# The first mixer's rotation without a product, and inverse-sum rows by transposition, in a two-block transformer kernel

## The chip, the cores and the metric

The kernel is one program on one core of a Trainium2 chip. The metric is the time of one execution on the device in microseconds (us), the median over runs. One core has a tensor engine (PE, whose loads of stationary operands are listed apart as PEld), a vector engine (DVE), a scalar engine (ACT), GpSimd (POOL) and a sync engine (SP), which here issues the transfers between memories (DMAs). All engines take their instructions in order and wait for each other through semaphores.

## The reference

A transformer of two blocks works on 512 tokens of 1024 features, and on 256 context tokens in its first block. The first block has two layers, each an attention mixer with adaptive gains (adaLN); the second block has two layers, each a mixer and a convolutional feed-forward part. The change touches three mixers.

The first mixer (mixer_a) has 16 heads of 64 features that share four key/value heads. Queries and keys of the latent tokens are rotated; those of the context are not:

```python
def apply_rope(x, cos, sin):
    a1, a2, b1, b2 = jnp.split(x, 4, axis=-1)
    rot = jnp.concatenate([-a2, a1, -b2, b1], axis=-1)
    return x * cos + rot * sin

# mixer_a, for each block of 128 queries
s_loc = q . k (three key blocks, window of 128) * scale
s_ctx = q . kc (256 context keys, not rotated) * scale
p = softmax([s_loc, s_ctx, sink])
y = (p v * silu(g)) @ w_o
```

The second mixer (mixer_b, 16 heads, latent attention) and the first mixer of the second block (even_mixer, 8 heads of 64 beside a linear recurrence) end in a division of each query's output by its row sum of exponentials; the kernel does it after the product with V.

## The kernel before

Matrices are kept transposed, with features on the 128 rows (partitions) and tokens on columns. Each float32 operand of a large product is split into a high and a low part (fp32r), and a product is three products of parts (`gemm_T`). Products that are not split are float32 products and stand in the trace as two records each.

The planner of the language orders each engine's instructions itself, by priority (the order of the program text) and by its own estimate of when operands are ready; buffers and PSUM banks go by tags. In the first mixer the banks are two for projections ("pj"), two for transpositions ("tp"), three for scores ("S") and one for outputs ("po").

`attn_a` (stage A1, about 64 to 412 us of the trace) is the first mixer. `g_k(pr)` and `g_q(t)` project a pair of heads for 512 latent tokens (bank `px`) and 256 context tokens (bank `pc`); both are pj banks, so a projection takes both. `rope` (line 559) rotates `px`: with a matrix `rot` ACT copies px to SBUF (`sw`), PE multiplies `sw` by the constant 128x128 matrix `rot` into a tp bank, and DVE multiplies that by the sine table, `sw` by the cosine table, and adds. Without a matrix (mixer_b and even_mixer, whose rotated partners lie 64 rows apart) ACT copies each half of 64 rows of px to the other half, and DVE multiplies px by the cosines, the copy by the signed sines, and adds. The result is split into `tH` and `tL` (128x768), of which SP moves the rows of each head by DMA (`dcopy`, line 591) into `Q` or `K`: in `g_q` two DMAs of 64 rows for each of two heads, in `g_k` four. `rope` is called 10 times in `attn_a`: for two pairs of keys and eight of queries. `head_a` then makes scores, softmax, transposed probabilities and outputs; `merge` interleaves a head's scores, the outputs of the head before, and projections (`g_q`, `g_g`, `g_v`, and chunks of the adaLN weights, `ada_...`) that fill PE in between and take pj banks as well.

`rows` (line 613) turns four columns of inverse row sums [128, 1] into rows [64, 128]: four float32 products whose stationary operand is the column repeated 64 times and whose moving operand is the identity. `head_b` (stage B3, about 590 to 800 us) calls it once for each of 16 heads, and `head_e` through `o_sum` (stage E, about 940 to 1050 us) once for each of 8. DVE reads the result from the tp bank.

`dhead` (line 600), used by even_mixer, moves one head out of a tile whose rotated halves lie 64 rows apart: two DMAs of 32 rows.

Of the kernel before, what the change touches and what calls it, by code (L numbers as in the profile page):

```python
# [43 lines left out]
# ---------------------------------------------------------------- host layout  # L44
def _tiles(w, groups):
    """[K, N] -> one [128, K/128 * 128] block per group of columns (features of a chunk on rows)."""
    kc = w.shape[0] // P
    w3 = w.reshape(kc, P, w.shape[1])
    return np.stack([np.ascontiguousarray(w3[:, :, g].transpose(1, 0, 2)).reshape(P, -1) for g in groups])


def _nat(w, ksub, cols):
    """[K, N] -> blocks [128, ksub * cols], ordered column chunk, then rows."""
# [23 lines left out]
def _rotmat(d, n):  # L77
    """lhsT of the axial rotation: out[m] = sum_p r[p, m] q[p]."""
    r = np.zeros((d, d), np.float32)
    q = d // 4  # L80
    for a, b in ((0, 1), (2, 3)):
        for i in range(q):
            r[b * q + i, a * q + i] = -1.0
            r[a * q + i, b * q + i] = 1.0
    return np.kron(np.eye(n, dtype=np.float32), r)


def _halves(d, n, axial):
    """order of the columns of n heads of d features in which each rotated pair lies n * d / 2 columns apart."""
    q = d // 4  # L90
    one = np.arange(d).reshape(2, 2, q).transpose(1, 0, 2) if axial else np.arange(d).reshape(2, 1, 2 * q)
    return (one.reshape(2, 1, d // 2) + d * np.arange(n)[None, :, None]).reshape(-1)


def _rope_rows(c, s, n, axial):
    """cos and signed sin tables [n * d, 2 S] for columns in that order."""
# [6 lines left out]
def _consts():  # L103
# [7 lines left out]
    c["rope_a"] = np.concatenate([np.tile(ca.T, (2, 1)), np.tile(sa.T, (2, 1))], 1)  # L111
    c["rot_a"] = _rotmat(64, 2)
# [20 lines left out]
def _layout(x):  # L133
# [12 lines left out]
    a["a_k"] = _tiles(w, [1024 + np.arange(P * i, P * i + P) for i in range(2)])  # L146
    a["a_v"] = _nat(w[:, 1280:1536], 4, 256)
    a["a_q"] = _tiles(w, pair)
# [63 lines left out]
# ---------------------------------------------------------------- the program  # L212
def blk(x, b):
    """token block b of a transposed operand, kept whole or as two halves."""
# [15 lines left out]
def some(g, n):  # L230
    """the next n steps of g."""
# [5 lines left out]
def skew(gs, lag=2):  # L237
    """Second halves of the generators some turns after the first ones."""
# [12 lines left out]
def mix(*gs):  # L251
    """Interleave generators; a third one (projections) takes four steps to the others' one."""
# [18 lines left out]
class Prog:  # L271
# [16 lines left out]
    # ---- small wrappers  # L288
# [18 lines left out]
    def bcast(self, ap, pool, n, tag, bufs=1):  # L307
        """[n] in DRAM -> [128, n]."""
# [4 lines left out]
    def gemm_T(self, W, toks, off=0, kc=8):  # L313
        """out^T tiles: weights stationary; toks: [(X, n, psum ap)]."""
# [8 lines left out]
    def gemm_first(self, srcs, pss, X, ahead=50):  # L323
        """The first output tiles of a phase, in halves of the tokens: the first half needs only the
        first two blocks, and goes ahead of the last block's norm."""
# [7 lines left out]
    def rstd(self, ms, n=1):  # L333
        """(ms)^-0.5 on [128, n]."""
# [4 lines left out]
    def sq(self, x, ss, f):  # L339
        """mean square of half f of a [128, 1024] tile's rows."""  # L340
# [5 lines left out]
    def row_r(self, x, ss=None):  # L346
        """1 / rms of a [128, 1024] tile's rows."""
# [7 lines left out]
    def norm_T(self, x, X, b, ps, acol, bcol=None, ss=None):  # L355
        """x: [128, 1024] token block -> columns of block b of X = (H list, L list), by a gain alone (a row
        of features on all partitions) or by gain and shift columns; the last step, out of the transposes,
        is left to the next call, so that its chain goes first."""
# [37 lines left out]
    def turn(self, n=0):  # L396
        """the transposes of norm_T that are open, but for the last n."""
# [21 lines left out]
    def out_proj(self, W, nch, X, nblk, ps, consume, first=None, late=0, begun=None):  # L419
        """natural out: activations stationary, weights moving; W[g * nch + i] = [128, 2k, 512]."""  # L420
# [33 lines left out]
    # ---- adaLN columns  # L454
# [28 lines left out]
    def ada_chunk(self, l, c, pm, row=0, full=None, fs=()):  # L483
        """512 columns; parts H, L of c go to rows row, 32 + row, those of c_ctx to 64 + row, 96 + row.
        Some chunks go unsplit by float32 products with full, where the tensor engine has the time."""
# [21 lines left out]
    def ada_cols(self, l, half, ps, tag, pool, full=None, fs=()):  # L507
        """gain and shift columns of half of the features, for the latents and the context."""
# [23 lines left out]
    def ada_grow(self, l, c, ps, tag):  # L532
        """rows of half a gate, added to the tile that holds the rows of all of them."""
# [10 lines left out]
    def ada_gates(self, l, c, ps, gates):  # L544
        """half c of the gates: [two [128, 512] halves for the latents (and the context)]."""
# [12 lines left out]
    # ---- pieces shared by the attentions  # L558
    def rope(self, ps_q, pool, tab, rot=None):
        """psum [128, 512] -> rotated [128, 512] f32 in SBUF; partners lie 64 rows apart, or come by a product  # L560
        with the constant rot."""
        nc = self.nc
        sw = self.t(pool, [P, S], F32, "tmp", 3)
        if rot is not None:
            self.act(sw, ps_q)
            pr = self.bank("tp")
            self.mm(pr, rot, sw, start=True, stop=True)
            t2 = self.t(pool, [P, S], F32, "tmp", 3)
            nc.vector.tensor_mul(t2, pr, tab[:, S:])
            nc.vector.tensor_mul(sw, sw, tab[:, :S])  # L570
            nc.vector.tensor_add(sw, sw, t2)
            return sw
# [16 lines left out]
    def dcopy(self, out, in_):  # L589
        """f32r rows moved between partitions."""  # L590
        self.nc.sync.dma_start(out.bitcast(F32), in_.bitcast(F32))

    def pv(self, po, cols, v, pH, pL, kb, last):
        """P V of key block kb into columns cols: rows 0-63 (V's high part) and 64-127 are to be added."""
# [1272 lines left out]
```

## Time and profile before

| | |
|---|---|
| median of 3 runs | 2120.14 us (2115.47 to 2120.24) |
| span of the profiled execution | 2120.9 us |
| PE busy | 2046.0 us, 96% |
| DVE busy | 1294.2 us, 61% |
| ACT busy | 1055.6 us, 50% |
| DMA engines | 34.1% of 16 engines' span |

The page gives no time of the profiled execution besides its span. The span is 0.8 us above the median of the runs. The busy time of PE includes the modelled ends of pipelined products, so 96% does not say that PE is at its peak.

### The profile page before, as it was taken

To read this page: it belongs to the slowest core of one execution; us is meant where nothing else is said; L and a number is where in the kernel's file an instruction comes from. 1 tells how busy PE (TensorE), PEld (TensorE's weight loads), DVE (VectorE), ACT (ScalarE), POOL (GpSimd) and SP (SyncE) were. 2 spreads that over 40 slices of the span, in tenths; PEclk is the share of its full clock that TensorE was granted. 3 is DMA by queue.
4 is the path that set the end of the run, shared out by engine and by line. 5 is a ranking of instruction groups with operands and counts; after the bars stand their busy time and mean duration, and the time that the engine had idled before them with its cause. 6 is when DMAs were issued, how large, how long until landed. Compare 5 with 4: busy or idle time off the path is not lost.

```text
span 2120.9 us, 28788 instructions
## 1 busy us (share of the span) xinstructions
PE 2046.0 (96%) x10609; PEld 1692.5 (80%) x10609; DVE 1294.2 (61%) x2491; ACT 1055.6 (50%) x2044; POOL 74.4 (4%) x162
## 2 busy tenths in 40 slices
PE   7899999998999999999999999999999999999998
PEld 4778888777788877867778888887888878888886
DVE  5588788847488886657756444423666775444323
ACT  5377677725367664555534333322566754333321
POOL 2100000000000000000000000000000000000000
PEclk9999999999999999999999999999999999999999
DMA  7344423322334332232123222222565532322222
GB/s 261 102 129 135 115 85 91 113 82 78 120 91 109 86 95 80 94 100 60 40 100 109 100 100 95 95 95 84 138 158 153 139 119 100 100 100 93 96 95 84
DMA packets 80893, 223.65 MB, mean 105 GB/s; under 512 B 13408, under 2 KB 19312, under 8 KB 80752
## 3 DMA queue, kind: packets, MB, share of 16 engines
q1 hardware_dynamic: 80752, 221.81, 34.1%
q8 instruction: 84, 1.38, 0.3%
q14 instruction: 57, 0.47, 0.1%
HBM read 176.67 MB, written 4.19 MB: 85 GB/s over the span
## 4 chain that ended last, share of the span: by engine, by line
PE 82%; DVE 7%; ACT 5%; issue 2%; DMA 2%; POOL 2%; SPq 0%; POOLq 0%; ACTq 0%; DVEq 0%
PE pj L293 33%; PE S L293 28%; PE po L293 13%; PE tp L293 2%; DVE wL L304 2%; PE tp L1305 1%; PE tp L1100 1%; POOL rstd L336 1%; ACT wH L290 1%; DVE XL L584 1%; ACT tmp L290 1%; ACT junk L290 1%; PE tp L1786 1%; PE tp L375 1%; DVE nm L1293 1%
## 5 line engine op out<-in xcount | busy, mean ns | idle before, releaser
L304 DVE TENSOR_TENSOR wL<-raw,wH 128x1024 fp32r<-128x1024 f32 (+2 forms) x291 | 353.9, 1220 | 461.7 <-ACT wH L290 449.1
L290 ACT ACTIVATE wH<-raw 128x1024 fp32r<-128x1024 f32 (+2 forms) x291 | 305.5, 1053 | 540.8 <-PE S L293 216.1
L293 PE MATMUL pj<-XH,wH 128*128 128x512 f32 (+1 forms) x672 | 260.5, 391 | 3.8 <-ACT tmp L290 1.3
L293 PE MATMUL pj<-XL,wH 128*128 128x512 f32 (+1 forms) x672 | 259.9, 390 | 0.1
L293 PE MATMUL pj<-XH,wL 128*128 128x512 f32 (+1 forms) x672 | 257.6, 386 | 0.5 <-DVE wL L304 0.5
L293 PE MATMUL S<-K,Q 96*128 96x384 f32 (+4 forms) x864 | 190.7, 330 | 4.5 <-ACT P L290 3.1
L293 PE MATMUL S<-XH,wH 128*128 128x512 f32 (+1 forms) x456 | 170.2, 374 | 1.0 <-ACT wH L290 1.0
L293 PE MATMUL S<-XH,wL 128*128 128x512 f32 (+1 forms) x456 | 169.9, 373 | 0.5 <-DVE wL L304 0.5
L293 PE MATMUL S<-XL,wH 128*128 128x512 f32 (+1 forms) x456 | 170.0, 373 | 0.0
L293 PEld LDWEIGHTS S<-K,Q 128*128 128x128 f32 (+1 forms) x864 | 141.8, 189 | 20.2 <-ACT P L290 7.2
L293 PEld LDWEIGHTS pj<-XH,wH 128*128 128x128 f32 x672 | 127.0, 189 | 29.7 <-ACT wH L290 2.7
L293 PEld LDWEIGHTS pj<-XH,wL 128*128 128x128 f32 x672 | 127.1, 190 | 23.3 <-issue 1.2
L293 PEld LDWEIGHTS pj<-XL,wH 128*128 128x128 f32 x672 | 127.4, 190 | 22.7 <-issue 1.8
L290 ACT ACTIVATE PTH<-tp 128x512 fp32r<-128x512 f32 (+2 forms) x192 | 91.2, 480 | 40.4 <-PE tp L1100 15.7
L584 DVE TENSOR_TENSOR PTL<-tp,PTH 128x512 fp32r<-128x512 f32 (+2 forms) x192 | 103.4, 542 | 9.3 <-ACT PTH L290 8.4
L293 PEld LDWEIGHTS S<-XH,wH 128*128 128x128 f32 x456 | 86.1, 189 | 16.4 <-ACT wH L290 1.7
L293 PEld LDWEIGHTS S<-XH,wL 128*128 128x128 f32 x456 | 86.3, 189 | 16.0 <-DVE wL L304 1.0
L293 PEld LDWEIGHTS S<-XL,wH 128*128 128x128 f32 x456 | 86.3, 189 | 15.1
L290 ACT ACTIVATE XH<-tp 128x512 fp32r<-128x512 f32 x128 | 75.1, 596 | 43.3 <-PE tp L375 24.0
L584 DVE TENSOR_TENSOR XL<-tp,XH 128x512 fp32r<-128x512 f32 x128 | 86.7, 684 | 10.6 <-ACT XH L290 9.5
L290 ACT ACTIVATE P<-S,nm 128x768 f32<-128x768 f32 (+1 forms) x96 | 72.5, 757 | 31.4 <-DVE nm L1018 12.2
L293 PE MATMUL po<-PTH,V 128*128 128x256 f32 (+1 forms) x224 | 79.0, 356 | 2.2 <-ACT PTH L290 2.0
(482 smaller groups left out, 4519.3 us busy)
## 6 DMA issues: line engine op xcount, KB each, us to landing
raw<-in_up SPq DMA_DIRECT2D x88, 512.0 KB, 3.4
raw<-in_ada SPq DMA_DIRECT2D x48, 512.0 KB, 4.3
raw<-in_dn SPq DMA_DIRECT2D x44, 512.0 KB, 3.4
raw<-in_o_o SPq DMA_DIRECT2D x11, 512.0 KB, 3.8
x<-in_x SPq DMA_DIRECT2D x8, 512.0 KB, 9.1
raw<-in_a_q SPq DMA_DIRECT2D x8, 512.0 KB, 4.6
raw<-in_a_g SPq DMA_DIRECT2D x8, 512.0 KB, 3.7
raw<-in_a_o SPq DMA_DIRECT2D x8, 512.0 KB, 3.5
```

Of the source, the lines that this page charges most:

```text
L290: self.nc.scalar.activation(out, in_, func, **kw)
L293: self.nc.tensor.matmul(out, l, r, start=start, stop=stop, **kw)
L304: nc.vector.tensor_sub(L[:, :n], raw[:, :n], H[:, :n].bitcast(F32))
L336: self.nc.gpsimd.tensor_tensor(r, ms, self.c_mh[:, :n], op=ALU.pow)
L375: nc.tensor.transpose(tp[:, kk, :], xh[g][:, kk * P:(kk + 1) * P], self.ident)
L584: self.nc.vector.tensor_sub(L, src, H.bitcast(F32))
L1100: nc.tensor.transpose(tp[:, (i - i0) * P:(i - i0 + 1) * P], Ps[i][0][:, at(i) * P:(at(i) + 1) * P], self.ident)
L1293: nc.vector.tensor_reduce(nm[:, i:i + 1], Sp[:, :, :384], axis=AX.XY, op=ALU.min)
L1305: nc.tensor.transpose(tp[:, i * P:(i + 1) * P], Ps[i][:, kb * P:(kb + 1) * P], self.ident)
L1786: nc.tensor.transpose(tp[:, (i - kb) * P:(i - kb + 1) * P], Ps[i][0][:, kb * P:(kb + 1) * P], self.ident)
```

## The change

The columns of the first mixer's query and key weights are reordered on the host, so that the partners of each rotated pair come out 64 rows apart, as in the other two rotated mixers; the table `rope_a` is laid out for that order, with the sign in the sine part. `rope` loses its branch with the matrix, and the constant `rot_a` and its DMA go. `g_k` and `g_q` move heads by `dhead`, so that each DMA of 64 rows becomes two of 32 rows. `rows` calls the transposition of PE where it called a product with the identity. Comments and docstrings are removed as well.

```diff
-    c["rope_a"] = np.concatenate([np.tile(ca.T, (2, 1)), np.tile(sa.T, (2, 1))], 1)
-    c["rot_a"] = _rotmat(64, 2)
+    c["rope_a"] = _rope_rows(ca, sa, 2, True)
...
-    a["a_k"] = _tiles(w, [1024 + np.arange(P * i, P * i + P) for i in range(2)])
+    ro = _halves(64, 2, True)
+    a["a_k"] = _tiles(w, [1024 + P * i + ro for i in range(2)])
-    a["a_q"] = _tiles(w, pair)
+    a["a_q"] = _tiles(w, [p[ro] for p in pair])
...
-    def rope(self, ps_q, pool, tab, rot=None):
+    def rope(self, ps_q, pool, tab):
         nc = self.nc
         sw = self.t(pool, [P, S], F32, "tmp", 3)
-        if rot is not None:
-            self.act(sw, ps_q)
-            pr = self.bank("tp")
-            self.mm(pr, rot, sw, start=True, stop=True)
-            t2 = self.t(pool, [P, S], F32, "tmp", 3)
-            nc.vector.tensor_mul(t2, pr, tab[:, S:])
-            nc.vector.tensor_mul(sw, sw, tab[:, :S])
-            nc.vector.tensor_add(sw, sw, t2)
-            return sw
         for z in (0, 64):
             self.act(sw[z:z + 64], ps_q[64 - z:128 - z])
         qs = self.t(pool, [P, S], F32, "tmp", 3)
...
         bc = self.bank("tp")
         for i in range(n):
-            self.mm(bc[0:64, i * P:(i + 1) * P], r[:, i:i + 1].to_broadcast([P, 64]), self.ident, start=True, stop=True)
+            self.nc.tensor.transpose(bc[0:64, i * P:(i + 1) * P], r[:, i:i + 1].to_broadcast([P, 64]), self.ident)
         return bc
...
-        rot = self.t(pool, [P, P], F32, "rot", 1)
-        nc.sync.dma_start(rot, I["rot_a"])
...
-            kf = self.rope(px, pool, rope, rot)
+            kf = self.rope(px, pool, rope)
...
-                        self.dcopy(k2[64 * hf:64 * hf + 64, i, :], src[64 * e:64 * e + 64, :])
+                        self.dhead(k2[64 * hf:64 * hf + 64, i, :], src, e)
...
-            qf = self.rope(px, pool, rope, rot)
+            qf = self.rope(px, pool, rope)
...
-                self.dcopy(q2[0:64, :], qH[64 * e:64 * e + 64, :])
-                self.dcopy(q2[64:128, :], qL[64 * e:64 * e + 64, :])
+                self.dhead(q2[0:64, :], qH, e)
+                self.dhead(q2[64:128, :], qL, e)
```

## Rows read from the trace of the kernel before

**Rows 1.** The page: chain that ended last, share of the span by engine and line

```profile
PE 82%; DVE 7%; ACT 5%; issue 2%; DMA 2%; POOL 2%; SPq 0%; POOLq 0%; ACTq 0%; DVEq 0%
```

**Rows 2.** Stretches: length, busy us (instructions) PE PEld DVE ACT POOL, clock, DMA, GB/s

```profile
260.00:280.00 20.00, 20.00 (x120) 17.39 (x118) 17.04 (x41) 13.56 (x32) 0.83 (x3) 1.00 0.25 69
...
590.00:800.00 210.00, 204.82 (x1214) 172.62 (x1213) 179.63 (x276) 145.95 (x290) 0.00 (x0) 1.00 0.37 95
...
940.00:1050.00 110.00, 107.38 (x663) 85.02 (x662) 81.64 (x212) 65.88 (x166) 2.72 (x3) 0.97 0.20 58
```

**Rows 3.** Chain within stage B3 (590 to 800 us), share by line

```profile
by line: PE S L293 22.4%; PE po L293 19.6%; PE tp L1305 14.7%; PE pj L293 11.9%; PE tp L293 7.7%; DVE nm L1293 5.2%; ACT tmp L290 3.4%; DVE XL L584 2.9%; issue 2.9%; ACT P L290 2.7%; DVE tmp L1321 2.3%; ACT XH L290 1.7%; DVE OT L1322 1.3%; 
```

**Rows 4.** PE groups, forms apart: out<-in, shape, count, busy us, mean ns, idle before

```profile
L293 PE MATMUL tp<-ident,l 128*64 128x128 f32 x128 | 18.0, 280 | 0.0
...
L293 PE MATMUL tp<-tmp,rot 128*128 128x512 f32 x20 | 10.8, 624 | 1.3 <-ACT tmp L290 1.3
L293 PE MATMUL tp<-ident,rl 128*64 128x128 f32 x64 | 10.2, 300 | 0.0
```

**Rows 5.** Timeline of PE at one call of rows in B3: start, duration, instruction

```profile
656.64 0.40 PE L293 MATMUL po<-XL,V 128*128 128x512 f32 x1
656.97 1.09 PE L293 MATMUL tp<-ident,l 128*64 128x128 f32 x8
...
658.33 0.34 PE L293 MATMUL S<-K,Q 96*128 96x384 f32 x1
```

**Rows 6.** Timeline of PE at four transpositions in B3

```profile
604.88 0.34 PE L293 MATMUL S<-K,Q 96*128 96x384 f32 x1
...
605.07 0.60 PE L1305 MATMUL tp<-ident,P 128*128 128x128 f32 x4
...
605.74 0.40 PE L293 MATMUL pj<-cqH,wL 128*128 128x512 f32 x1
```

**Rows 7.** Timeline of weight loads: a 32-column transposition (L1158) behind a 128-column one

```profile
511.48 0.14 PEld L1157 LDWEIGHTS tp<-ident,xhc 128*128 128x128 f32 x1
511.54 0.10 PEld L1158 LDWEIGHTS tp<-ident,xhc 128*32 128x32 f32 x1
```

**Rows 8.** Timeline of PE at one rotation product in A1

```profile
139.37 0.34 PE L293 MATMUL po<-PTL,V 128*128 128x384 f32 x1
139.55 0.34 PE L293 MATMUL po<-PTH,V 128*128 128x384 f32 x1
139.84 1.10 PE L293 MATMUL tp<-tmp,rot 128*128 128x512 f32 x2
...
141.01 0.40 PE L293 MATMUL pj<-wL,adast 128*128 128x512 f32 x1
141.25 0.39 PE L293 MATMUL pj<-wH,adast 128*128 128x512 f32 x1
```

**Rows 9.** Timeline of DVE and ACT at another rope in A1

```profile
274.57 1.23 DVE L304 TENSOR_TENSOR wL<-raw,wH 128x1024 fp32r<-128x1024 f32 x1 [0.92 <-ACT wH L290]
274.70 0.59 ACT L290 ACTIVATE tmp<-pj 128x512 f32<-128x512 f32 x1
```

**Rows 10.** DVE's cosine product without a matrix, ACT's copies: ns min/median/max

```profile
L576 DVE TENSOR_TENSOR tmp<-pj,rope_e x5: 681/690/691, 916.7 to 1019.6; 128x512 f32<-128x512 f32 x5
...
L290 ACT ACTIVATE tmp<-pj x31: 577/590/624, 65.5 to 1073.2; 64x512 f32<-64x512 f32 x16, 128x512 f32<-128x512 f32 x15
```

**Rows 11.** SP's issues: 64-row DMAs in A1, 32-row DMAs in E

```profile
84.28 1.11 SPq L591 DMA_DIRECT2D Q<-tL  x2
...
953.03 1.15 SPq L591 DMA_DIRECT2D Q<-tH  x2
```

**Rows 12.** What PE waited for, 64 to 412 us: total us, times, longest

```profile
PE tp L293 <- ACT tmp L290: 1.3, 1, 1.3
```

**Rows 13.** Around a fall of the granted clock in A1: PE's gap, and the stretch behind

```profile
241.61 1.05 PE L293 MATMUL tp<-sel,sgx 128*128 128x2 f32 x8 [0.96 <-ACT sgx L290]
...
244.00:248.00 4.00, 4.00 (x18) 3.39 (x17) 3.28 (x8) 3.12 (x6) 0.00 (x0) 0.61 0.17 41
```

More of the change, by code (lines that the diff above doesn't have):

```diff
@@ L74, in _axial @@
     return np.cos(ang).astype(np.float32), np.sin(ang).astype(np.float32)
[L77 to L85, printed above, removed]
 def _halves(d, n, axial):
```

## The prediction

> **What bounds the kernel now.** I read the page's chain first: most of the span is on PE [rows 1]. Then the stages that the change touches, by stretches [rows 2]: in A1 PE is busy in all of a 20 us stretch, in B3 in 204.8 of 210 us, in E in 107.4 of 110, at the full granted clock or near it. DVE comes second: 85% of A1's stretch, 179.6 of 210 us in B3, 74% of E. So PE is the bound, but with little room above DVE in A1 and B3. The chain within B3 says the same in another way: its PE lines make up 76%, DVE and ACT take turns for most of the rest, and the line "tp L293" (7.7% of 210 us, 16.2 us, about 1.0 us for each of 16 heads) is the products of `rows` themselves: they lie on the chain [rows 3]. The time of a PE instruction can't be taken from its listed duration, which holds the modelled end; I take the distance between starts.
>
> **Rows by transposition.** The records tell the counts: 128 + 64 records, two for each float32 product, are 96 products in 24 calls, 16 in B3 and 8 in E [rows 4]. One call: from the start of the product ahead to the start of the second product behind are 658.33 - 656.64 = 1.69 us [rows 5]. Two products of 512 columns lie in that, at 0.24 us each from start to start [rows 8], so the call holds PE for 1.21 us. Its eight records start (1.09 - 0.28) / 7 = 0.12 us apart, some 0.93 us in all; the rest is a gap ahead and behind. Four transpositions of the same moving operand, measured in the same way, take 605.74 - 604.88 = 0.86 us less a product of 384 columns (0.18 us) and one of 512, so 0.44 us [rows 6, 8]. The difference is 0.77 us a call and 24 x 0.77 = 18.5 us (12.3 in B3, 6.2 in E). No row shows a transposition whose stationary operand is a repeated column of 64. The bounds: if the gaps stay, four records of 0.11 us go, 0.44 us a call, 10.6 us; if it went on as two passes, nothing. A loss I exclude, since it would take more than the two passes of today. I take 0.77, because the nearest row, a transposition with 32 columns, is loaded 0.06 us behind the load before it, without a gap [rows 7]. DVE reads the same bank, with the same instruction.
>
> A rule speaks against this. By the rows, the granted clock is full in B3, where 24 transpositions a head already stand among the products [rows 2]; where it fell in A1, PE had stood idle for 0.96 us and then done eight products of two columns [rows 13]. The Trainium skill (TensorE: Matmul & The Clock Gate, Part 4: PE-mode transpose) says that the full clock doesn't engage in transpose mode. By that rule the call would come at half clock, and drag its neighbours; the trace of B3 disagrees. It is a rival below.
>
> **The rotation product goes.** 20 records are 10 products [rows 4]. One takes 141.01 - 139.55 = 1.46 us less a product of 384 and one of 512 columns, 1.04 us [rows 8]; 10 x 1.04 = 10.4 us. PE also waited for ACT's copy of px once for 1.3 us ahead of a rotation product [rows 12]. DVE's work stays at three instructions of 0.69 us [rows 10]. ACT gets one more copy, 0.59 us, since 64 rows take as long as 128 [rows 10]: 5.9 us, hidden while ACT has a third of A1's stretch free [rows 2]; on the chain they would cost all of it.
>
> What moves is the bank. Before, px was free after ACT's copy; now it is read by two copies and by DVE's cosine product. In another rope the copy ends at 275.29 [rows 9]. Now the second ends at 275.88, DVE comes out of a weight's low part at 275.80, and its product of 0.69 us ends near 276.5: px is free 1.2 us later. In five of the ten places the product right behind the rotation is the first of an adaLN chunk, which needs a pj bank (one of the five is shown) [rows 8]. There 1.2 us of bank takes the place of 1.04 us of product. What hides it is attention work: scores and transpositions of two heads, which the planner may put there; without that cover PE gains nothing in these five. I take nothing for five and 1.04 for five: 5.2 us, with ends of 0 and 11.7 us.
>
> **Twice the DMAs of heads.** In A1 the 64-row DMAs number 2 x 8 for keys and 8 x 4 for queries, 48; they become 96 of 32 rows. SP takes 1.11 us for two of 64 rows and 1.15 for two of 32 [rows 11], so it takes 0.57 us per DMA whatever the rows: 48 x 0.57 = 27 us more SP work. Each pair of heads comes 2.3 us later, and so do the weight loads queued behind on SP, on which ACT's and DVE's splits and then PE wait; for a pair of keys it is 4.6 us. The bounds are 0 and 27 us. I take 0: a head's queries are made while the head before is worked on, and the list of PE's waits over A1 names no DMA of Q or K, its longest entry being the copy [rows 12]. The DMA of `rot` itself goes, off the path.
>
> **Sum.** All of PE's cuts give 18.5 + 10.4 = 28.9 us. In B3, without 12.3 us, DVE's 179.6 us would be 91% of 198 us; a quarter of its chain is on DVE and ACT already [rows 3]. So I let four fifths of the cut in B3 and E come through: 14.8 us. With 5.2 us from A1 it is 20.0 us. The profiled span is 2120.9 us and has no other time around it; it stands 0.8 us above the median of 2120.14. So 2120.9 - 20.0 - 0.8 = 2100.1 us; I say 2100.
>
> **Rivals.** (a) PE paces everything: 28.9 us and the wait of 1.3, 2120.1 - 30.2 = 2090. For it: PE busy in all of A1's stretch [rows 2]. Against: DVE at 85% beside it. (b) A1 gains nothing or loses by the bank: the 1.2 us of the later release come through at all ten ropes, 12 us, and take more than the product's 10.4; with 14.8 from `rows` that is 2120.1 - 14.8 + 1.6 = 2107, and 2110 where ACT's extra copies delay other work by half their 5.9 us. For it: DVE comes free just when px needs it [rows 9], and at 85% busy it often won't be. Against: five places have no projection right behind. (c) The transposition doesn't do what is said, and the repeated column keeps its gaps or its two passes: 0.8 x 10.6 = 8.5 us or 0 in place of 14.8, so 2106 to 2115. Against: the 32-column load without a gap [rows 7]. (d) Slower: the weight loads in A1 come late behind the doubled DMAs on SP, and the whole 27 us goes through ACT's and DVE's splits to PE: 2120.1 - 20.0 + 27.4 = 2127.5. It decides from the point where 1.7 of the 2.3 us of each pair come through, which would need that the next weights are never loaded ahead. For it: SP issues one DMA after another [rows 11]. Against: PE's waits name no DMA [rows 12]. (e) Slower by the rule on transpositions: a fall of 1.6 us at each of 24 calls costs 38 us (4 us at 0.61) [rows 13], less the 20.0, so 2138. Against: B3's full clock [rows 2].
>
> **Chances.** Forecast 0.42, (a) 0.24, (b) 0.17, (c) 0.09, (d) 0.05, (e) 0.03. The forecast's own range is 2094 to 2106. The range wanted reaches to most of (a) and (b) and the first end of (c): 2087 to 2114. 0.3% (6.4 us, about what a measurement of this kernel can tell from no change) puts the bounds at 2113.8 and 2126.5. Faster: all of the forecast and of (a), most of (b) and two thirds of (c), 0.85. Same: the rest of (b) and (c) and a little of (d), 0.09. Slower: the rest, 0.06.
>
> **What the profile after would show.** The line "tp<-ident,l" with half its records, a call of 0.44 us between its neighbours, B3 shorter by about 10 us at a full clock, E by 5: if the call keeps 0.8 us, (c). No "tp<-tmp,rot"; A1 shorter by about 5 us: if by 10, the bank was covered; if by nothing, look in PE's waits for DVE's cosine product (bank) or for "wH" behind a DMA (SP). Longer waits for weights in A1 would be (d), half-clock stretches in B3 (e). The prediction is wrong if the planner's new order of all engines moves stages that the change doesn't touch, which no row can price.

## The result, and the profile after

The kernel after takes 2136.2 us in the median (2131.72 to 2138.61), the one before 2119.77 beside it: a ratio of 1.0072, with an interval of 1.0059 to 1.0086. Run again beside the experiments it took 2132.03, a ratio of 1.0041 (1.0023 to 1.0059). The prediction said 2100 us and faster; the kernel became slower by 11 to 16 us. Its profile below is of an execution of 2138.61 us.

The stretches of the kernel after, first B3, then E (both lie 18 us later than before), then ten microseconds of A1. Columns as in [rows 2]: length, busy us of PE, PEld, DVE, ACT, POOL, granted clock, share and rate of the DMAs.

```profile
608.00:818.00 210.00, 200.63 (x1169) 168.40 (x1168) 182.38 (x281) 147.99 (x296) 0.00 (x0) 1.00 0.36 94
958.00:1068.00 110.00, 106.09 (x606) 82.93 (x605) 77.48 (x202) 62.00 (x160) 2.39 (x2) 0.91 0.20 58
284.00:288.00 4.00, 2.62 (x10) 1.25 (x8) 3.94 (x6) 1.69 (x2) 0.00 (x0) 1.00 0.47 132
288.00:294.00 6.00, 5.31 (x22) 4.53 (x23) 2.98 (x15) 2.99 (x9) 0.18 (x1) 0.55 0.79 227
```

PE is less busy in B3 (200.63 us of 210 against 204.82) and DVE more (182.38 against 179.63). In E the granted clock is 0.91 in the mean where it was 0.97. In A1, where it was full from 280 to 320 us, there is now a stretch near 0.5, the lower level of 1.2 GHz; of the four microseconds ahead of it PE had stood idle for 1.4. The chain that ended last, from the page, has three points of its share less on PE than before [rows 1] and DVE, ACT and issue one more each:

```profile
PE 79%; DVE 8%; ACT 6%; issue 3%; DMA 2%; POOL 2%; SPq 0%; POOLq 0%; ACTq 0%; DVEq 0%
```

The call of `rows` did what was forecast. The timeline of PE at one call in B3 of the kernel after:

```profile
673.33 0.39 PE L282 MATMUL po<-XL,V 128*128 128x512 f32 x1
673.56 0.60 PE L596 MATMUL tp<-ident,l 128*64 128x128 f32 x4
673.91 0.48 PE L282 MATMUL pj<-cqH,wH 128*128 128x512 f32 x1
674.26 0.50 PE L282 MATMUL po<-XH,V 128*128 128x512 f32 x1
```

From start to start, as in the prediction, 674.26 - 673.33 = 0.93 us less two products of 0.24 us: 0.45 us, where 0.44 was forecast and 1.21 was measured before [rows 5]. Half the records are there, and no rotation product is left [rows 4]:

```profile
L596 PE MATMUL tp<-ident,l x64: 270/272/275, 620.2 to 813.9; 128*64 128x128 f32 x64
L596 PE MATMUL tp<-ident,rl x32: 270/272/421, 989.7 to 1066.2; 128*64 128x128 f32 x32
```

These lines also date the stages (first to last instruction). B3 takes 193.7 us where it took 198.0, so the change gained there; but it begins 17.8 us late. E's calls span 76.5 us and spanned 74.3. The loss is made ahead of B3. The scores of A1 show most of it (L282, the first and the last instruction of the group):

```profile
L282 PE MATMUL S<-K,Q x288: 274/283/668, 100.1 to 408.1; 128*128 128x256 f32 x96, 128*128 128x384 f32 x32, 128*128 128x512 f32 x16
```

Before they ran from 89.4 to 396.2 us: A1's attention begins 10.7 us late and ends 11.9 us late. (The other 5.9 us of the 17.8 are lost between A1 and B3, in stages that the change doesn't touch; the section on the prediction comes back to them.) What PE waited for in A1 (64 to 425 us) in the kernel after: total us, times, longest:

```profile
PE pj L282 <- DVE tmp L555: 6.9, 6, 2.8
PE pj L282 <- DVE wL L293: 3.3, 5, 1.1
PE pj L282 <- DVE V L563: 2.8, 3, 0.9
...
PE pj L282 <- ACT wH L279: 1.6, 4, 0.5
```

The first is the bank, held until DVE's cosine product (L555) has read it; before it did not occur, and two waits for ACT's copy were 1.3 us each (one of them stands in [rows 12]). The second and fourth are weights: 4.9 us together, where the kernel before had 0.8 for `wL` and 1.2 for `wH`. No line names a DMA, as before.

### The profile page after: what moved, and what is told of

It reads as the page before. It is cut to its first block, busy times and chain, and to the rows that moved or that the text cites. A ratio compares the mean times of both kernels' runs of the same rounds, so it can differ in the third digit from the quotient of the medians.

```text
span 2136.8 us, 28608 instructions
## 1 busy us (share of the span) xinstructions
PE 2043.9 (96%) x10493; PEld 1688.9 (79%) x10493; DVE 1293.1 (61%) x2491; ACT 1061.3 (50%) x2054; POOL 73.5 (3%) x162
## 4 chain that ended last, share of the span: by engine, by line
PE 79%; DVE 8%; ACT 6%; issue 3%; DMA 2%; POOL 2%; SPq 0%; POOLq 0%; ACTq 0%; DVEq 0%
PE pj L282 32%; PE S L282 29%; PE po L282 12%; DVE wL L293 2%; ACT wH L279 1%; PE tp L1282 1%; POOL rstd L325 1%; PE tp L1077 1%; ACT P L279 1%; DVE XL L563 1%; ACT junk L279 1%; ACT tmp L279 1%; PE tp L364 1%; PE tp L282 1%; PE tp L1763 1%
## 5 line engine op out<-in xcount | busy, mean ns | idle before, releaser
L282 PE MATMUL pj<-XH,wH 128*128 128x512 f32 (+1 forms) x672 | 260.9, 391 | 5.5 <-DVE tmp L555 3.4
L282 PE MATMUL pj<-XL,wH 128*128 128x512 f32 (+1 forms) x672 | 259.2, 389 | 0.1
L282 PE MATMUL pj<-XH,wL 128*128 128x512 f32 (+1 forms) x672 | 258.9, 388 | 0.1
L282 PE MATMUL S<-K,Q 96*128 96x384 f32 (+4 forms) x864 | 193.4, 335 | 5.8 <-ACT P L279 4.7
L282 PE MATMUL S<-XH,wH 128*128 128x512 f32 (+1 forms) x456 | 170.0, 373 | 1.0 <-ACT wH L279 1.0
L282 PE MATMUL S<-XH,wL 128*128 128x512 f32 (+1 forms) x456 | 170.0, 373 | 0.5 <-DVE wL L293 0.5
L282 PE MATMUL S<-XL,wH 128*128 128x512 f32 (+1 forms) x456 | 170.0, 373 | 0.0
L282 PEld LDWEIGHTS S<-K,Q 128*128 128x128 f32 (+1 forms) x864 | 143.4, 192 | 23.2 <-ACT P L279 11.8
L282 PEld LDWEIGHTS pj<-XH,wH 128*128 128x128 f32 x672 | 127.6, 190 | 31.4 <-DVE tmp L555 4.1
L282 PEld LDWEIGHTS pj<-XH,wL 128*128 128x128 f32 x672 | 127.7, 190 | 23.9 <-issue 2.0
L282 PEld LDWEIGHTS pj<-XL,wH 128*128 128x128 f32 x672 | 127.6, 190 | 22.7 <-issue 1.2
L282 PEld LDWEIGHTS S<-XH,wH 128*128 128x128 f32 x456 | 86.2, 189 | 16.6 <-ACT wH L279 1.7
L282 PEld LDWEIGHTS S<-XH,wL 128*128 128x128 f32 x456 | 86.3, 189 | 16.1 <-DVE wL L293 1.0
L282 PEld LDWEIGHTS S<-XL,wH 128*128 128x128 f32 x456 | 86.1, 189 | 15.0
L563 DVE TENSOR_TENSOR XL<-tp,XH 128x512 fp32r<-128x512 f32 x128 | 86.6, 685 | 10.7 <-ACT XH L279 9.9
L279 ACT ACTIVATE P<-S,nm 128x768 f32<-128x768 f32 (+1 forms) x96 | 72.5, 758 | 34.1 <-DVE nm L995 15.7
L282 PE MATMUL po<-PTH,V 128*128 128x256 f32 (+1 forms) x224 | 79.2, 357 | 4.4 <-ACT PTH L279 4.2
```

Of the source, the lines that this page charges most:

```text
L279: self.nc.scalar.activation(out, in_, func, **kw)
L282: self.nc.tensor.matmul(out, l, r, start=start, stop=stop, **kw)
L563: self.nc.vector.tensor_sub(L, src, H.bitcast(F32))
```

## The experiments

Each was timed in five rounds beside the kernel before, whose median was 2120.0 to 2121.3 us in these jobs. "Scores" are the first and last of A1's score products in the profile; "clock" is the median of the executions' mean granted clocks. The kernel before has 89.4 to 396.2 and 0.990, the kernel after 100.1 to 408.1 and 0.984.

| kernel | median us | ratio (interval) | scores us | clock |
|---|---|---|---|---|
| rows_only | 2113.4 | 0.9968 (0.9957-0.9980) | 89.9-396.4 | 0.989 |
| rope_only | 2135.5 | 1.0069 (1.0053-1.0084) | 100.1-406.3 | 0.987 |
| dma32_only | 2128.8 | 1.0044 (1.0028-1.0060) | 96.7-400.8 | 0.988 |
| after_dma64 | 2117.0 | 0.9982 (0.9972-0.9991) | 87.2-393.5 | 0.987 |
| after_kq | 2124.8 | 1.0019 (1.0007-1.0031) | 95.7-399.9 | 0.987 |
| after_early | 2119.8 | 0.9993 (0.9984-1.0003) | 96.7-398.0 | 0.987 |
| rope32 | 2128.6 | 1.0036 (1.0019-1.0052) | 88.1-402.4 | 0.986 |
| kpack | 2129.4 | 1.0043 (1.0028-1.0058) | 100.5-400.0 | 0.986 |
| kq_early | 2117.2 | 0.9982 (0.9971-0.9993) | 98.2-396.2 | 0.987 |
| dma64_early | 2117.6 | 0.9979 (0.9968-0.9989) | 88.7-395.3 | 0.987 |
| rows_b3 | 2111.9 | 0.9950 (0.9936-0.9963) | 89.4-396.0 | 0.991 |
| after_again | 2132.0 | 1.0041 (1.0023-1.0059) | 97.3-408.4 | 0.987 |
| after_2q | 2118.4 | 0.9986 (0.9977-0.9994) | 89.3-394.6 | 0.987 |
| dma32_2q | 2120.6 | 0.9992 (0.9981-1.0002) | 87.4-391.9 | 0.989 |

### Each part alone

rows_only, the kernel before with the transposition (in the code of this section `...` and shortened lines stand for what doesn't matter here):

```
-  self.mm(bc[...], r[:, i:i + 1].to_broadcast([P, 64]), self.ident, start=True, stop=True)
+  self.nc.tensor.transpose(bc[...], r[:, i:i + 1].to_broadcast([P, 64]), self.ident)
```

> The kernel before with nothing changed but the transpositions in rows (24 calls). In the changed kernel a call holds PE for 0.41 us in place of 1.21 between its neighbours, yet stage B3 became 4.3 us shorter and the stretch from E's first to its last transfer of output weights 4.5 us longer. Theory (A1 alone makes the kernel slower; the cut of rows is mostly handed back as waits of PE in B3): 2112 to 2119, B3 shorter by 3 to 6 us, E no more than 3 us longer. Rival (the transpositions themselves make the later stages slower): 2123 or more, with E longer by at least 4 us. Rival of the prediction (full cut comes through): 2105 or less.

rope_only, the kernel after with the float32 product back in `rows` (the reverse of that diff):

> The changed kernel with the four float32 products of rows put back, so that only the first mixer's rotation, its weight order and its DMAs of 32 rows differ from before. Theory: A1 carries all of the loss, first transfer of the mixer's output weights 12 us later than before, total 2132 to 2138. Rival (rows makes it slower): at most 2124.

dma32_only, the kernel before with each transfer of 64 rows as two of 32:

```
-  self.dcopy(q2[0:64, :], qH[64 * e:64 * e + 64, :])
+  for z in (0, 32):
+      self.dcopy(q2[z:z + 32, :], qH[64 * e + z:64 * e + z + 32, :])
...
```

> The kernel before with each 64-row DMA of a head in the first mixer as two DMAs of 32 rows; the rotation product stays. Theory of the doubled DMAs (they hold the single buffers tH and tL longer, so that the first queries come late): A1 6 to 9 us longer, 2126 to 2129. Rival theory (only the later release of the projection's bank px costs time): within 2 us of before, 2118 to 2122.

after_dma64, the kernel after with `dcopy` of 64 rows in place of `dhead` in A1:

> The changed kernel with DMAs of 64 rows as before: the rows of two heads are mixed, so queries and keys are not those of the reference, and the amount of work is that of the changed kernel with half the DMAs. Theory of the doubled DMAs: 6 to 9 us faster than the changed kernel, 2127 to 2130, first queries' DMAs issued at 82 to 85 us and not at 89.6. Rival (bank px alone): 2134 to 2138 with PE's waits for DVE's cosine product unchanged at 7 us. If both halves count, 2127 to 2130 with those 7 us still there.

The transposition is a gain of 6.6 us (2119.99 to 2113.39), a third of the 18.5 us that it takes from PE. All of the loss is in the first mixer's part: it alone costs 15.5 us. The transfers are the largest piece: with 64 rows the kernel after falls by 19.2 us (2136.2 to 2117.04; 15.0 from its second timing, 2132.03), more than I had expected; in the kernel before the doubling alone costs 8.8 us. What is left of the rotation's part, without its transfers, is not a gain: by the medians it is a loss of 3.6 us (2117.04 against 2113.39). The intervals of the two ratios overlap, so the size of that loss is not shown. Beside doubled transfers the same part costs 6.7 us (2135.5 in rope_only against 2128.8 in dma32_only). So the parts do not add up: the doubling costs 15 to 19 us without the rotation product (and with the transposition) and 8.8 in the kernel before.

### The start, the bank, the number of transfers

after_kq gives the first keys' parts other buffers, so that the first queries' parts needn't wait for the single ones:

```
-  kH = self.t(pool, [P, 768], F32R, "tH", 1)
-  kL = self.t(pool, [P, 768], F32R, "tL", 1)
+  kH, kL = (self.t(pool, [P, 768], F32R, *(("Q", 3) if pr == 0 else (n, 1))) for n in ("tH", "tL"))
```

> The kernel after, but for the first pair of keys, whose rounded and low parts go into two of the three buffers of the queries instead of the two single ones, so that the first queries' parts needn't wait for the keys' 16 transfers. Theory A (the doubled transfers cost where the first heads wait for them, and the late start is carried to the stage's end): first score product at 88 to 92 us instead of 100.1, first output-weight transfer of the stage 6 to 10 us earlier than 414.6, and 2125 to 2130 us against 2136.2, with a mean clock of 0.985 to 0.988. Theory B (the 48 added issues cost all along the stage on SyncE's queue): at most 3 us come back, 2133 to 2137.

after_early frees the bank after one read; the cosine product, too, reads the copy:

```
+  qs = self.t(pool, [P, S], F32, "tmp", 3)
+  self.act(qs, ps_q)
   for z in (0, 64):
-      self.act(sw[z:z + 64], ps_q[64 - z:128 - z])
+      self.act(sw[z:z + 64], qs[64 - z:128 - z])
-  nc.vector.tensor_mul(qs, ps_q, tab[:, :S])
+  nc.vector.tensor_mul(qs, qs, tab[:, :S])
```

> The kernel after, with one more copy in the first mixer's rotations: ACT copies the projection to SBUF whole, and the two swapped copies and the cosine product read that copy, so the projection's bank is free after one read instead of three. Theory A (the rotation product's gain was eaten by TensorE's waits for the bank that the cosine product holds): the 6.9 us of waits on the cosine product vanish, waits on the copy of 1 to 2 us take their place, and the time is 2129 to 2133 against 2136.2. Theory B (the bank is not what it waits for in the end; the waits move on to the next link of the chain, and 10 copies of 0.6 us lengthen it): 2135 to 2140.

rope32 keeps a pair within its head, 32 rows apart, so that 64-row transfers serve again, at the price of four copies of 32 rows out of the bank instead of two (the weights' columns and the table are laid out to match):

```
-  for z in (0, 64):
-      self.act(sw[z:z + 64], ps_q[64 - z:128 - z])
+  for z in range(0, P, 32):
+      self.act(sw[z:z + 32], ps_q[z ^ 32:(z ^ 32) + 32])
```

> The kernel after, with the rotated pairs 32 rows apart inside a head instead of 64 apart over two heads: four swapped copies of 32 rows in place of two of 64, and the transfers are those of 64 rows again, half as many. Theory A (the doubled transfers made the kernel slower, the removal of the rotation product did not): first score product at 88 to 92 us, 2115 to 2122 us, whatever the two further copies per rotation (some 0.6 us each on ACT) do to the bank. Theory B (the rotation without a product is slow by itself, by what it does to ACT and the bank): 2127 us or more, since it has more of that than the kernel after.

kpack puts rounded and low part in one tile, for keys and for queries, so that one transfer moves both for keys:

```
-  for i, src in enumerate((kH, kL)):
-      for hf in range(2):
-          self.dhead(k2[64 * hf:64 * hf + 64, i, :], src, e)
+  for hf in range(2):
+      self.dhead(k2[64 * hf:64 * hf + 64], kHL, e)
```

> The kernel after, with the rounded and the low part in one tile, so that one transfer of 32 rows moves both for the keys: 8 transfers of twice the bytes for each pair of keys, as many as in the kernel before; the queries' transfers stay doubled. Theory A (it is the number of the keys' transfers ahead of the first queries that makes the start late): first score product at 90 to 95 us, 2125 to 2131 us. Theory B (the queries' doubled transfers, 32 of the 48, carry the cost): first score product at 97 us or later and 2132 to 2137 us. Theory C (bytes behind one another, not issues, set the landing): as B, with keys landing no earlier than in the kernel after.

after_kq came in at 2124.8, 0.2 us below A's range; the first score came only to 95.7, not to 88 to 92. after_early went past its theory (2119.8 against 2129 to 2133): it gave back 12.2 us or more, where the waits for the bank had been 6.9, and why it gave more is not shown. The waits for the cosine product are gone, as the timelines of PE show early in A1; the bracket is the idle time ahead and what ended it. The kernel after:

```profile
68.35 0.50 PE L282 MATMUL pj<-XH,wH 128*128 128x512 f32 x1 [2.84 <-DVE tmp L555]
79.74 0.38 PE L282 MATMUL pj<-wH,xcH 128*128 128x256 f32 x1 [2.74 <-DVE tmp L555]
```

And with the early copy:

```profile
76.25 0.38 PE L282 MATMUL pj<-wH,xcH 128*128 128x256 f32 x1 [1.28 <-ACT tmp L279]
```

rope32 speaks for its theory B: the first score comes early (88.1), yet the scores end at 402.4 and the kernel takes 2128.6 us. Its bank is read by four copies and the product, and PE waits for L555 nine times, 15.7 us, against 6.7 us in after_dma64: 9.0 us more wait, 11.6 us more time, with 64-row transfers in both. The longer hold of the bank and the further copies on ACT that make it were not separated. kpack came 6.8 us below the kernel after's first timing with the first score no earlier (100.5), which would be theory A's time without its mechanism. But its ratio of 1.0043 is no lower than the 1.0041 of the kernel after in its second timing, so no gain is shown.

### Both mends, and the rotation without either cost

kq_early joins after_kq and after_early; dma64_early joins after_dma64 and after_early.

> The kernel after with both mends together: the first keys' parts in the queries' buffers, and the projection copied out of its bank whole before the rotation. Each alone gave back 11.4 and 16.4 us of the 16. Theory A (two causes at different places that add up, the late first heads and the bank): 2108 to 2114 us, under the kernel with the transpositions alone (2113.4), mean clock 0.988 or more. Theory B (both work through the same thing, the stage's late end, and what one gives back the other can't give again): 2117 to 2122 us.

> The kernel after with the whole copy out of the bank and with transfers of 64 rows, which mix rows of two heads in scores and outputs (a part of the computation that is changed; instructions and bytes stay). It shows what taking away the rotation product is worth once neither the bank nor the transfers stand against it, beside the kernel with the transpositions alone (2113.4 us). Theory A (TensorE bounds the stage, so ten products of 1.04 us less come through in part): 2105 to 2111 us. Theory B (TensorE's cut in this stage comes back as waits for ACT's and VectorE's links, as in the second mixer): 2112 to 2117 us.

Theory B in both, dma64_early 0.6 us beyond its range. The two mends do not add up: from 2136.2 they give 11.4 and 16.4 us alone and 19.0 together, from 2132.0 they give 7.2, 12.2 and 14.9. And with the transfers of 64 rows, freeing the bank gives nothing more (2117.6 against 2117.0). No kernel with the new rotation came below 2117 us; the transposition alone stands at 2113.4. Over 64 to 412 us, dma64_early has PE 331.78 us busy and rows_only 338.14, with DVE at 276.61 and 276.26:

```profile
64.00:412.00 348.00, 331.78 (x2016) 288.42 (x2016) 276.61 (x664) 252.62 (x527) 14.46 (x65) 0.99 0.37 106
```

Against rows_only:

```profile
64.00:412.00 348.00, 338.14 (x2037) 291.25 (x2035) 276.26 (x663) 240.03 (x506) 16.06 (x65) 0.99 0.37 106
```

PE has 6.4 us less to do in the same time, and the scores end 1.1 us earlier. The cut came back as idle time: A1 is paced as much by what ACT and DVE hand on as by PE.

### The queue

after_2q issues the second of each head's two transfers from GpSimd's queue; dma32_2q does the same in dma32_only (shortened):

```
-  self.dcopy(d, s_)
+  (self.nc.gpsimd if z else self.nc.sync).dma_start(d.bitcast(F32), s_.bitcast(F32))
```

> The kernel after, with the second of the two transfers of each head's rows issued from GpSimd's queue in place of SyncE's, so that SyncE issues as many as in the kernel before. Theory A (the issues on SyncE carry the cost, weight loads and first queries standing behind them): waits for weights in the first mixer fall from 3.3 to about 1 us, first score product at 88 to 95 us, time 2116 to 2124. Theory B (arrival of the halves and the changed order carry it): 2130 to 2137.

> The kernel before with each transfer of 64 rows in the first mixer split in two of 32, the second issued from GpSimd's queue. With both on SyncE's queue this cost 8.8 us. Theory A (SyncE's queue): 2119 to 2123 us. Theory B (arrival and order): 2127 to 2131 us.

Theory A in both: the 32-row transfers are all still there, and the cost is gone (2118.4 against 2136.2 or 2132.0; 2120.6 against 2128.8). With half of them off SP's queue the doubled transfers cost nothing that can be told: 2118.4 is 1.3 us above after_dma64, and 2120.6 is the time of the kernel before. The timeline of SP in the kernel after, at a pair of heads:

```profile
149.72 1.15 SPq L570 DMA_DIRECT2D Q<-tH  x2
151.06 1.14 SPq L570 DMA_DIRECT2D Q<-tL  x2
152.25 1.22 SPq L570 DMA_DIRECT2D Q<-tH  x2
153.52 1.23 SPq L570 DMA_DIRECT2D Q<-tL  x2
154.79 12.52 SPq L289 DMA_DIRECT2D raw<-in_ada  x4
171.50 0.33 SPq L289 DMA_DIRECT2D raw<-in_a_q  x1
```

And with half of them on the other queue:

```profile
145.93 1.19 SPq L570 DMA_DIRECT2D Q<-tH  x2
147.28 1.15 SPq L570 DMA_DIRECT2D Q<-tL  x2
148.47 12.01 SPq L289 DMA_DIRECT2D raw<-in_ada  x4
163.60 0.33 SPq L289 DMA_DIRECT2D raw<-in_a_q  x1
```

Eight issues hold SP from 149.72 to 154.79, 5.1 us; four hold it for 2.5. Behind them stand the weight loads, 6.3 us later in the one than in the other, and the next query weights 7.9 us later (part of that is lateness from earlier pairs). What it does to PE is to be seen some 16 us on, where the products of these weights stand in its timeline. In the kernel after:

```profile
170.27 0.50 PE L282 MATMUL pj<-wH,adast 128*128 128x512 f32 x1 [0.41 <-ACT wH L279]
171.53 0.50 PE L282 MATMUL pj<-wL,adast 128*128 128x512 f32 x1 [0.76 <-DVE wL L293]
...
172.93 0.49 PE L282 MATMUL pj<-wH,adast 128*128 128x512 f32 x1 [0.45 <-ACT wH L279]
174.19 0.50 PE L282 MATMUL pj<-wL,adast 128*128 128x512 f32 x1 [0.77 <-DVE wL L293]
```

In after_2q the same products run from 164.29 with one wait of 0.23 us. The releaser that PE names is the split of the weights on ACT or DVE; the transfer that was late is two links behind and appears in no list of PE's waits. Over A1 the waits for `wL` fall from 3.3 to 0.7 us, as theory A expected, and those for `wH` from 1.6 to 0.6; in the other pair `wL` falls from 3.4 to 0.8.

That is 3.6 us. The larger effect is at the start: the first score comes 10.7 us earlier (89.3 against 100.1). The last transfer of the first keys, ACT's first write of the first queries and their first transfer, in the kernel after:

```profile
78.99 2.50 SPq L570 DMA_DIRECT2D K<-tL  x4
...
88.42 0.38 ACT L279 ACTIVATE V<-pj 128x256 fp32r<-128x256 f32 x1 [3.65 <-PE pj L282]
88.70 0.38 ACT L279 ACTIVATE tH<-pj 128x256 fp32r<-128x256 f32 x1
...
89.62 1.78 SPq L570 DMA_DIRECT2D Q<-tH  x3
```

And in after_2q:

```profile
74.87 1.23 SPq L570 DMA_DIRECT2D K<-tL  x2
...
81.16 0.38 ACT L279 ACTIVATE tH<-pj 128x256 fp32r<-128x256 f32 x1
83.88 1.14 SPq L570 DMA_DIRECT2D Q<-tH  x2
```

The keys' transfers are out at 76.1 instead of 81.5 us, and the queries' parts go into the same single buffers `tH` and `tL` that these transfers read. But the planner has also put two copies of V ahead of the queries on ACT in the kernel after (84.39 and 88.42), which in after_2q stand behind them. So the other queue changes the planner's order together with SP's time, and what each of the two is worth is not separated.

### The transposition by stage, and the kernel after again

rows_b3 is the kernel before with the transposition in B3's 16 calls only.

> The kernel before with the transpositions in the second mixer only; the fourth stage's eight calls stay float32 products. Both places together gave 6.6 of 18.5 us less work of TensorE. Theory A (the gain is of the second mixer, and the fourth stage hands its 6.2 us back, since its order changes and its falls of the clock grow): 2110 to 2114 us. Theory B (each place gives its share, some 36% of its cut): 16 of 24 calls give 4.4, 2115 to 2117 us.

> The kernel after, unchanged, for more executions with their clocks beside the kernels of this job. The theory that its time is to a large part TensorE's clock, granted at 1.2 GHz more often: executions differ by 0.8 to 0.9 us for each us of lost clock (1 minus the mean granted clock, times the time), and its median clock lies under 0.986 where the kernel before has 0.990; time 2134 to 2138. The rival (the clock is a bystander): no relation between an execution's clock and its time, and the same 0.990.

rows_b3 is the fastest of all, 2111.9 us, 9.0 below the kernel before: B3 gives its gain, and nothing is to be seen of a gain by E's eight transpositions; by the medians they take 1.5 us back (the intervals of rows_b3 and rows_only just overlap). B3's calls of `rows` span 198.0 us before and 193.4 here, 4.6 us of the 12.3 that PE lost. Where the rest went is to be seen in the waits of its weight loads (600 to 798 us). Before:

```profile
PEld S L293 <- ACT P L290: 4.8, 9, 0.7
...
PEld tp L1305 <- DVE XL L584: 3.9, 10, 1.1
```

In rows_b3:

```profile
PEld S L293 <- ACT P L290: 9.7, 15, 1.4
PEld tp L1308 <- DVE XL L584: 8.3, 15, 1.4
```

9.3 us more waiting for ACT's exponentials and DVE's split, which overlaps other work in part: PE itself is idle for 4.3 us more over B3's calls (9.3 against 5.0). In E a fall of the clock comes in. Its calls span 74.3 us in rows_b3 and 76.6 in rows_only; the stretch from 1040 to 1044 us, first in rows_only:

```profile
1040.00:1044.00 4.00, 4.00 (x18) 3.44 (x17) 1.74 (x5) 1.74 (x4) 0.00 (x0) 0.50 0.00 0
```

and in rows_b3:

```profile
1040.00:1044.00 4.00, 4.00 (x33) 3.50 (x32) 3.46 (x10) 2.22 (x7) 0.00 (x0) 1.00 0.00 0
```

18 instructions against 33 in the same four microseconds: PE at 1.2 GHz, without having waited (0.2 us idle ahead). Just ahead of it rows_only had this on PE:

```profile
1034.03 0.62 PE L1530 MATMUL tp<-ident,ke 128*128 128x128 f32 x4
1034.49 0.60 PE L617 MATMUL tp<-ident,rl 128*64 128x128 f32 x4
...
1035.50 1.15 PE L293 MATMUL S<-i,kn 32*128 32x128 f32 x8 [0.18 <-ACT kn L290]
```

transpositions and small products of 32 rows. The stretch below full clock lasts some 8 us here and costs 3.4 us of lost clock (1 minus the granted clock, times the length), about half of E's 6.2; PE is also idle for 2 us more in E, and the rest is open. All eleven profiles with the transposition in E have this fall near the end of E's calls; none of the five with float32 products there has it (the kernel before, rope_only, dma32_only, dma32_2q, rows_b3). The order of the instructions there differs too, so whether it is the transposition or its new neighbours was not separated.

after_again: seven executions from 2122.95 to 2135.98 us; the median clock is 0.987, not under 0.986 as expected, and the time a little below its range. The relation to the clock holds. With the lost clock as (1 - clock) x time, over 132 executions of the 15 timings, each compared with the mean of its own, time rises by 0.83 us for each us of lost clock (correlation 0.91). That is a relation, and which of the two is the cause it does not say.

## Why the prediction was wrong, by its own steps

**Rows, size of a call.** Right: 0.45 us where 0.44 was forecast, and the loads of the repeated column carry no gap.

**Rows, what comes through.** Mis-sized: four fifths of 18.5, 14.8 us, were to come through, and 6.6 did. In B3 4.6 of 12.3 us shortened the stage. The prediction read a chain with 76% PE as PE's share of every cut (the lines of [rows 3] give DVE and ACT 19.5%, a fifth and not the quarter that it says); but with DVE at 86% beside it [rows 2, 3], the next links stand right behind, and their waits grew by 9.3 us. In E nothing of 6.2 us came through, and about half of it went with a fall of the clock at one place, which would be rival (e)'s mechanism in the other stage. In [rows 13], on which (e)'s price rests, the eight records are four float32 products and not eight. The Trainium skill's rule (TensorE: Matmul & The Clock Gate, Part 4: PE-mode transpose) that the full clock doesn't engage in transpose mode does not fit B3, whose clock stays 1.00 with more transpositions than before; it would fit E's stretch at 0.50, but there the order of the products changed as well.

**The rotation product.** Wrong in size and probably in sign: 5.2 us were to come, and by the medians the part costs 3.6 us when the transfers are left at 64 rows. The release 1.2 us later that the prediction worked out was there, as waits of up to 2.8 us, and rival (b) had this mechanism; but with the bank freed early it costs the same (dma64_early), so the bank is not the whole of it. The cut itself came back as PE's idle time: from 64 us to the last score PE is idle for 12.3 us in after_dma64's profile and 8.6 in that of rows_only. The lost clock is 26.7 us in the mean of after_dma64's executions and 23.7 in rows_only, at 0.83 a difference of 2.5 us, about the size of the loss; but the clocks are given to 0.001, which is 2.1 us. Where these falls come from was not settled; no one place is common to the profiles.

**The doubled transfers, the step that failed.** Taken at nothing with 27 us as the other end; 15.0 to 19.2 us by after_dma64, 13.7 to 17.8 by after_2q, 8.8 in the kernel before. Two reasons stood for the nothing. The first was that a head's queries are made while the head before is worked on. The first pair has no head before it: its queries wait for the keys' 16 transfers, and the first score is 10.7 us later than with half of them on the other queue. Giving the first keys other buffers (after_kq) brought back 7.2 to 11.4 us, with the waits for `wL` still at 3.3. The second was that PE's waits name no DMA [rows 12]. They name none now either; PE's waits name the split of the weights, and the transfer stands two links further back. Rival (d), weight loads behind the doubled issues on SP, came nearest and had a chance of 0.05; what is to be seen of it as waits of PE is 3.6 us, and the late first queries it did not name. The estimate of SP's time itself was right: eight issues take 5.1 us, four 2.5 [rows 11]. What the step left out is that SP's timeline shows one issue behind the other, the weight loads among them, so an issue that nobody waits for can still be late work for somebody.

**The rest.** (d) came out at 2127.5 because it kept 20.0 us of gains; with the gains measured (6.6 less 3.6) and 19.2 us of transfers the kernel after is 2119.99 - 6.6 + 3.6 + 19.2 = 2136.2. That sum closes by its making, since each term is the difference of two neighbouring runs. The terms depend on their order: the doubling costs 8.8 us in the kernel before, and each of four mends alone (early copy, other buffers, other queue, 64 rows) brings 7 us or more back, but no two together come below 2117 us. The early copy gives back 12.2 us or more with all the doubled transfers on SP's queue; so in the kernel after the queue costs that much only together with the bank's hold, and how the two work on each other is open.

**The share of the clock.** The kernel after lost 35.2 us of clock in its first four executions and 27.7 in the seven others, the kernel before 21.2. (The figures are medians of clock and time; means give 34.7, 28.3 and 21.7.) At 0.83 us each, 5 to 12 us of the 11 to 16 go with PE at 1.2 GHz, some of it behind the new waits, such as the stretch from 288 us above. A late weight would then be paid twice, once as waiting and once as slow products behind it. That is argued from the idle time ahead of the falls in A1, and not shown by an experiment that fills it.

**Stages that the change doesn't touch.** The prediction feared that a new order would move them. From the feed-forward part of the second block's first layer on (1085 us of the trace before) the instructions stand in the same order in both, and from the first call of `rows` in B3 to the end of the span the kernel after is 1.9 us shorter (1516.6 against 1518.5): the loss is all ahead of B3. It is not all A1's, though, in the profile above. The stretch from A1's last score to B3, in the kernel before, the kernel after and the kernel after again (its own profile, with every instruction of PE in the same order as in the first):

```profile
400.00:602.00 202.00, 188.31 (x898) 155.22 (x897) 122.81 (x241) 93.22 (x198) 7.19 (x12) 0.97 0.34 107
412.00:620.00 208.00, 193.11 (x898) 159.31 (x897) 122.92 (x241) 93.36 (x198) 7.19 (x12) 0.94 0.34 105
412.00:615.00 203.00, 187.56 (x901) 154.32 (x900) 123.20 (x241) 93.37 (x198) 7.20 (x12) 0.97 0.34 107
```

The same work took 5 to 6 us longer in one execution than in the others, at a lower clock. In the second profile A1's scores end 12.2 us late and B3 begins 12.8 us late: there A1 is nearly all of the loss. But A1's own order did change with every edit of A1, which is why single waits there can't be priced alone; how much the order itself costs stays open.

## What to carry to other kernels

Price each added issue on an in-order queue by what stands behind it there, above all weight loads, and not by whether an engine's list of waits names a transfer: follow each "waits for a split" one link further, to the load that the split waited for. Ask of the first piece of a stage, too, what hides its transfers: it has no piece before it. A cut on the engine with the largest busy share gives only the distance to the next one; with another at 85% beside it, a third came through here and not four fifths. Before doubling small transfers, look for a second queue: here it took a few lines and gave back what the doubling cost.

## What the hardware showed that was not expected

The clock fell with hardly any idle time ahead of it: in E it went to 0.50 behind 5 us of transpositions and products of 32 rows in which PE waited 0.2 us. The same program, with every instruction in the same order, took 208 us at a mean clock of 0.94 in one execution and 203 at 0.97 in another for the stretch from A1 to B3. An issue of a transfer between partitions mostly held SP for 0.57 to 0.63 us at 32 rows (1.14 us for two to 2.50 for four) and for 0.55 us at 64 (1.11 for two), while on GpSimd's queue a pair of 32 rows took 0.98 to 1.22 us.
